# Chunk attention that takes 512 queries at once for each block of keys, with the score work moved to other steps

## The chip, the cores and the metric

The kernel runs on one core of one Trainium2 chip. The metric is the time of one execution on the device, in microseconds (us). Of three timed executions of the kernel before, the median is 1950.27 us (1949.37 to 1955.56); a fourth execution was taken with the hardware profiler and is the one whose trace is read below.

Engines are named as in the profile: PE is the matrix engine (PEld its loading of stationary operands), DVE, ACT and POOL are the vector, scalar and general engines, SP issues most of the transfers. Each works through its own queue in order, and waits there on semaphores.

## The reference, cut to what matters

One layer of a streaming encoder for 2048 positions of width 1024, all in float32: RMSNorm, one wide input projection, two gated branches (chunk-causal attention with 8 heads of 64; retention with 8 heads), a gated merge, an output projection and a final RMSNorm. The change is in the attention alone. Per head, a query in chunk n (chunks of 64) sees the keys of chunks n-8 to n:

```
dist = q_local[:, None] + N_LEFT_CHUNKS * CHUNK - p[None, :]
bias = rel_bias[:, clip(dist, -REL_CLIP, REL_CLIP) + REL_CLIP]
s = einsum('nqhd,nkhd->nhqk', qc, k_band) * scale + bias[None]
s = where(valid, s, NEG_INF)
w = softmax(s, axis=-1)
o = einsum('nhqk,nkhd->nqhd', w, v_band)
```

So a tile of 128 queries (two chunks) sees at most 640 keys, that is five blocks of 128; a block of 128 keys is seen by five such tiles in a row, at most four of which lie in one block of 512 queries.

## The kernel before, in words

**Precision.** Every float32 operand is split into a high and a low part of type fp32r ("h" and "l" in the names), and a product is two or three matmuls on the parts. In the attention a score tile is two matmuls per range of columns (`wide` from `qa` and `ka`, whose rows hold both parts), and the product of weights and values is two (`po` from `pth` and from `ptl`, both with the stationary operand `va`, in which the value's two parts stand side by side).

**Stages.** Projection of the first 1024 positions, attention and retention of the first half (`heads(0)`), projection of the second half, `heads(1)`, then merge and output. Between the attention's and the retention's own matmuls the program puts dense projection work: `fill(n)` takes n steps of a stream of dense work, and a step is three matmuls of 512 columns (`ps_g_...` in the trace of attention). `later(n, fn)` hands the rest of a task to the n-th step from now, where it is emitted ahead of that step's matmuls. So the order in every engine's queue is the order in which this program emits, and no scheduler changes it.

**Attention before.** `attention(s, ...)` runs once per half. Its unit is a head h, a block b of 512 positions and a half `un` of 256 queries: 32 units in each call. A unit does:

- `soft` twice (a = 0, 1), each for 128 queries: the scores go into one of two places in the PSUM tile `wide` (three banks of 512 columns; columns 128 to 767 and 768 to 1407, so the middle bank holds some of each). Then `least` one step later (DVE: bias added and the minimum taken, result in `pr`, row minimum in `mn`), `exps` two steps later (ACT: exponential and row sum), `normed` four steps later (DVE reciprocal, POOL scales `pr`). `pr` has four buffers (`PR_BUFS`).
- `weighted` for the unit before: three groups of two key blocks each. A group transposes the 128x128 pieces of `pr` on PE (`tp`, one of four PSUM banks that the dense work uses too), copies them to `pth` (ACT), writes the rest to `ptl` (DVE, a step later), and three steps later (`PV_LAG`) multiplies: per key block, values stationary, 256 columns of weights moving, for `pth` and `ptl`. Of the six key blocks the first and the last are seen by one of the two query tiles only, and there the other 128 columns of `pth` and `ptl` are set to zero on DVE.
- after a block's second half, `out_`: ACT copies the low half of `po` to `oa`, DVE adds the high half, POOL multiplies with the gate `ua`, and SP stores it. `po` is one bank.

The order of a unit is: scores a = 0, two steps, scores a = 1, one step, then group, step, group, step, group, step of the unit before. For block 0 there are no earlier keys: one group and two groups, and scores of 128 to 512 columns.

Loads are issued by SP (`load_q`, `load_k`, `load_vs`, `load_u`), one unit ahead for the queries. Tiles of the pool `e` (`E(...)`: `qa`, `va`, `ua`, `pth`, `ptl`, `oa`) share twelve buffers (`E_ATT`); a tile waits until the one that had its buffer is no longer used.

The functions that the change touches, with the line numbers of the profile (instructions recorded through a helper have its line, L143, in the trace):

## Time and profile before

| | us |
|---|---|
| timed executions, median (range) | 1950.27 (1949.37 to 1955.56) |
| the profiled execution, own time | 1955.26 |
| its span, first to last instruction | 1953.5 |
| PE busy in the span | 1889.6 (97%) |
| PEld / DVE / ACT / POOL busy | 1624.6 / 1358.5 / 931.6 / 971.0 |
| attention of the first half, first scores to last product | about 354 to 568 |
| attention of the second half | about 1102 to 1349 |

The columns of the views: a row of the timeline has the start and the busy time in us, the engine, the line, the operation, out<-in by the program's names, the shape of the output and how many instructions of one kind follow each other. Matmuls are pipelined: a matmul's shown time is longer than the distance to the next one, so what a matmul costs is read from the starts of neighbouring rows. A gap shorter than that overlap does not show up as idle time. In a row of a group, the count is followed by busy time and mean duration, and by the engine's idle time just before such instructions with what ended it.

### The profile page before, as it was taken

How to read it: one execution, taken by the hardware profiler on the slowest of the kernel's cores; microseconds unless marked ns; L12 is line 12 of the kernel's file. 1: busy time of each engine (PE TensorE's matmuls, PEld its weight loads, DVE VectorE, ACT ScalarE, POOL GpSimd, SP SyncE). 2: the span in 40 equal slices, each digit the busy share in tenths (PEclk: the TensorE clock that was granted, in tenths of full speed). 3: DMA queues.
4: the chain of work that ended last, by engine and by line, in shares of the span. 5: the costliest groups of instructions: out<-in, count | busy, mean ns of one | idle time of the engine just before them, and what ended most of it. 6: DMA issues, size and time to landing. Idle time of an engine off the chain costs nothing. (4 is left out here: it accounts for less than half of the span.)

```text
span 1953.5 us, 31945 instructions
## 1 busy us (share of the span) xinstructions
PE 1889.6 (97%) x10437; PEld 1624.6 (83%) x10437; DVE 1358.5 (70%) x2473; ACT 931.6 (48%) x1931; POOL 971.0 (50%) x790
## 2 busy tenths in 40 slices
PE   7999989999999999999989999999999999999998
PEld 6889879888888887799879888888888878887886
DVE  6878788677766558888788677765455655557655
ACT  7545554566655445343333566664455321223554
POOL 0425545555545565535455454554554114557775
PEclk9999999999999999999999999999999999999999
DMA  6585976656559978665765555654999899977673
GB/s 194 154 259 194 283 251 212 195 173 187 168 161 282 277 226 278 201 224 181 221 226 190 178 158 164 179 162 134 267 273 275 302 370 333 313 265 246 205 233 134
DMA packets 325557, 435.93 MB, mean 223 GB/s; under 512 B 29880, under 2 KB 191184, under 8 KB 325392
## 3 DMA queue, kind: packets, MB, share of 16 engines
q1 hardware_dynamic: 260096, 368.35, 58.9%
q10 hardware_dynamic: 65296, 65.55, 11.0%
q8 instruction: 83, 1.36, 0.3%
q14 instruction: 82, 0.67, 0.1%
HBM read 288.14 MB, written 145.64 MB: 222 GB/s over the span
## 5 line engine op out<-in xcount | busy, mean ns | idle before, releaser
L143 POOL TENSOR_SCALAR pr<-pr,rsum 128x640 f32<-128x640 f32 (+4 forms) x128 | 96.1, 751 | 212.5 <-DVE ptl L143 104.9
L143 PE MATMUL ps_g_z<-r,wh_g 128*128 128x512 f32 x448 | 145.3, 406 | 1.9 <-DVE c_g L143 1.9
L143 PE MATMUL ps_g_x<-r,wh_g 128*128 128x512 f32 x448 | 144.6, 404 | 1.0 <-ACT u_g L143 0.9
L143 DVE CUSTOM_DVE_ANT_0 pr<-wide,bt 128x640 f32<-128x640 f32 (+4 forms) x128 | 94.2, 736 | 61.8 <-PE wide L143 53.6
L143 ACT ACTIVATE pr<-pr,mn 128x640 f32<-128x640 f32 (+4 forms) x128 | 98.0, 766 | 80.9 <-DVE mn L143 80.9
L143 DVE TENSOR_TENSOR ptl<-tp,pth 128x384 fp32r<-128x384 f32 x168 | 96.0, 572 | 41.5 <-ACT pth L143 39.0
L143 ACT CAST pth<-tp 128x384 fp32r<-128x384 f32 x168 | 84.5, 515 | 68.2 <-PE tp L143 65.3
L143 POOL TENSOR_TENSOR sl<-sm,sh 128x384 fp32r<-128x384 f32 x64 | 68.2, 1065 | 62.9 <-ACT sh L143 44.8
L143 ACT CAST wh_p<-raw_p 128x512 fp32r<-128x512 f32 x111 | 68.3, 619 | 63.1 <-PE ps_p_v L143 16.6
L143 DVE TENSOR_TENSOR wl_p<-raw_p,wh_p 128x512 fp32r<-128x512 f32 x111 | 91.5, 835 | 8.7 <-ACT wh_p L143 8.7
L143 POOL TENSOR_TENSOR wl_g<-t_g,wh_g 128x512 fp32r<-128x512 f32 x56 | 75.1, 1341 | 39.5 <-ACT wh_g L143 39.2
L143 PEld LDWEIGHTS tp<-ident,pr 128*128 128x128 f32 x560 | 71.1, 140 | 27.6 <-POOL pr L143 3.1
L143 DVE TENSOR_TENSOR sm<-sr,dm 128x384 f32<-128x384 f32 x64 | 35.5, 555 | 82.8 <-PE sr L143 28.5
L143 PE MATMUL po<-pth,va 128*128 128x256 f32 x336 | 92.4, 295 | 0.0
L143 PE MATMUL tp<-ident,pr 128*128 128x128 f32 x560 | 89.3, 272 | 3.0 <-POOL pr L143 1.7
L143 PE MATMUL wide<-ka,qa 128*128 128x384 f32 (+1 forms) x448 | 88.2, 313 | 2.2 <-DVE mn L143 2.1
L143 PEld LDWEIGHTS wide<-ka,qa 128*128 128x128 f32 x448 | 74.6, 188 | 18.6 <-DVE mn L143 8.7
L143 PE MATMUL po<-ptl,va 128*128 128x256 f32 x336 | 88.3, 284 | 1.4 <-DVE ptl L143 0.2
L143 PE MATMUL ps_g_z<-r,wl_g 128*128 128x512 f32 x224 | 89.0, 397 | 0.0
L143 PE MATMUL ps_g_x<-r,wl_g 128*128 128x512 f32 x224 | 88.8, 397 | 0.0
L143 PEld LDWEIGHTS ps_g_x<-r,wh_g 128*128 128x128 f32 x448 | 76.8, 191 | 10.8 <-ACT u_g L143 2.3
L143 PEld LDWEIGHTS ps_g_z<-r,wh_g 128*128 128x128 f32 x448 | 76.6, 191 | 10.4 <-issue 2.3
(930 smaller groups left out, 6293.5 us busy)
## 6 DMA issues: line engine op xcount, KB each, us to landing
raw_g<-in_w_in_dram ACTq DMA_DIRECT2D x56, 512.0 KB, 4.6
raw_p<-in_w_in_dram ACTq DMA_DIRECT2D x50, 512.0 KB, 5.7
qa<-qas SPq DMA_DIRECT2D x128, 128.0 KB, 3.4
qr<-qrs SPq DMA_DIRECT2D x128, 128.0 KB, 4.9
vr<-vrs SPq DMA_DIRECT2D x64, 256.0 KB, 5.4
ka<-kas SPq DMA_DIRECT2D x56, 256.0 KB, 3.3
va<-vas SPq DMA_DIRECT2D x40, 256.0 KB, 3.5
kds<-kdt_k SPq DMA_DIRECT2D x32, 256.0 KB, 3.9
```

The lines of the kernel that those rows point to most:

```text
L143: return tc.keep_in_program_order(op(*a, **k))
```

## The change

The unit of attention becomes a head and a whole block of 512 queries, 16 units in each call. The product of weights and values is done per key block for all query tiles that see it: with t the query tile (0 to 3) and j the key block (0 to 7, block 4 being the first of the unit's own positions), block j is seen by the tiles from max(0, j-4) to min(3, j), so its moving operand is 1, 2, 3, 4, 4, 3, 2, 1 pieces of 128 columns wide, and nothing is set to zero. Six groups: j = (0, 1), 2, 3, 4, 5, (7, 6), of 3, 3, 4, 4, 3, 3 transposes. For block 0 only the last three groups exist.

A unit is written as twelve slots, each followed by one step. Even slots hold a group of the current unit; slots 2, 6, 8 and 10 (`SOFT_AT`) hold the scores of the next unit's four tiles. The queries' first half for the next unit is loaded in slot 0 and the second in slot 3, keys two units ahead in slot 6, values and gate in slot 9. For a unit of block 0, slots 0, 1 and 4 have no step, and the unit before the first has none in slots 0 and 1. The first group's product comes four steps after its transposes, the others' three. `pr` has five buffers and is allocated at `least`, the pool `e` has eleven. The number of steps is the same as before: 198 in the first call, 222 in the second.

```diff
-E_ATT = 12
+E_ATT = 11
-PR_BUFS = 4
+PR_BUFS = 5
+SOFT_AT = (2, 6, 8, 10)
...
-        units = [(h, b, un) for h in range(HEADS) for b in (2 * s, 2 * s + 1) for un in range(2)]
+        units = [(h, b) for h in range(HEADS) for b in (2 * s, 2 * s + 1)]
...
-        def soft(h, b, un, a):
+        def soft(h, b, t):
...
-            pr = sbp.tile([P, WIN], F32, tag="pr", bufs=PR_BUFS, name=f"pr_{nm}")
...
             def least():
+                prs[h, b, t] = sbp.tile([P, WIN], F32, tag="pr", bufs=PR_BUFS, name=f"pr_{nm}")
...
-        def weighted(h, b, un, pr2):
...
+        def weighted(h, b, gr):
+
+            k0 = 0 if b > 0 else 4
+            js = ((0, 1), (2,), (3,), (4,), (5,), (7, 6))[gr]
+            tp = ACC(f"tp_{h}_{b}_{gr}")
+            c, cut, parts = 0, [], []
+            for j in js:
+                ts = range(max(0, j - 4), min(4, j + 1))
+                cut.append((j, c, ts))
+                for t in ts:
+                    at = (j - max(t, k0)) * P
+                    pe.transpose(tp[:, c:c + P], prs[h, b, t][:, at:at + P], ident)
+                    c += P
...
+            def product():
+                for j, at, ts in cut:
+                    n = len(ts) * P
+                    v4 = vts[h, b - 1 + j // 4][:, j % 4, :]
+                    for i, p in enumerate(parts):
+                        pe.matmul(
+                            po[:, ts[0] * P:ts[0] * P + n], v4, p[:, at:at + n],
+                            start=j == (0 if b > 0 else 4) and i == 0, stop=gr == 5 and j == 6 and i == 1,
+                            skip_group_check=True,
+                        )
+                if gr == 5:
+                    later(1, out_)
...
+            part("h")
+            later(1, lambda: part("l"))
+            later(PV_LAG + (gr == 0), product)
+
+        def slot(m, n):
+
+            if n == 0 and m + 1 < len(units):
+                h, b = units[m + 1]
+                load_q(h, b, 0)
...
+            if n == 3 and m + 1 < len(units):
+                load_q(*units[m + 1], 1)
+            if n == 6 and m + 2 < len(units):
+                load_k(*units[m + 2])
+            if n == 9 and m + 1 < len(units):
+                load_vs(*units[m + 1])
+                load_u(*units[m + 1])
+            if m >= 0 and n % 2 == 0:
+                weighted(*units[m], n // 2) if units[m][1] or n > 4 else None
+            if m + 1 < len(units) and n in SOFT_AT:
+                soft(*units[m + 1], SOFT_AT.index(n))
...
+        fill(2)
+        for m in range(-1, len(units)):
+            for n in range(12):
+                slot(m, n)
+                bare = (0, 1) if m < 0 else () if units[m][1] else (0, 1, 4)
+                fill(0 if n in bare else ATT_FILL)
+        fill(PV_LAG + 3)
```

Counted over the whole program, PE's queue loses 224 of its matmuls (`po` from 336 + 336 to 224 + 224) and DVE's loses 224 settings to zero; the count of every other kind of instruction is unchanged. Two places show how the order moves.

On PE, the product of one group in the second half: in the kernel before, block 3, first half of the queries, third group's transposes and the first group's product behind them.

```order
L143 MATMUL tp_3_0_2_14597<-ident,pr_3_1_14455 128x128
L143 MATMUL tp_3_0_2_14597<-ident,pr_3_0_14418 128x128
L143 MATMUL tp_3_0_2_14597<-ident,pr_3_1_14455 128x128
L143 MATMUL po<-pth_3_0_0_14567,va_2_14330 128x256
L143 MATMUL po<-ptl_3_0_0_14575,va_2_14330 128x256
L143 MATMUL po<-pth_3_0_0_14567,va_2_14330 128x256
L143 MATMUL po<-ptl_3_0_0_14575,va_2_14330 128x256
```

In the changed kernel, from the transposes of block 2's fifth group (`tp_2_4`) on: the scores of the next unit's third tile, then the product of the fourth group.

```order
L144 MATMUL tp_2_4_13789<-ident,pr_2_2_13609 128x128
L144 MATMUL tp_2_4_13789<-ident,pr_2_3_13648 128x128
L144 MATMUL wide<-ka_3_13559,qa_3_1_13718 128x384
L144 MATMUL wide<-ka_3_13559,qa_3_1_13718 128x256
L144 MATMUL wide<-ka_3_13559,qa_3_1_13718 128x384
L144 MATMUL wide<-ka_3_13559,qa_3_1_13718 128x256
L144 MATMUL po<-pth_2_3_13765,va_2_13622 128x512
L144 MATMUL po<-ptl_2_3_13775,va_2_13622 128x512
L144 MATMUL ps_g_3_z<-r_86,wh_g_3_4_13611 128x512
```

Two matmuls of 512 columns stand where four of 256 stood, and between a group's transposes and its product there is now the next pair of slots, scores included.

On DVE, the two minima (`ISA pr...<-wide,bt`) whose scores follow each other most closely: before, with what stands between them,

```order
L143 ISA pr_2_0_14629,mn_2_0_14630<-wide,bt_14200 128x640
L143 ISA mn_2_0_14630 128x1
L143 TENSOR_TENSOR c_g_4_14641<-ps_g_4_z,u_g_4_14561 128x512
L143 TENSOR_TENSOR wl_g_5_0_14579<-raw_g_5_0_14150,wh_g_5_0_14578 128x512
L143 SCALAR_TENSOR_TENSOR g_3_2_1_14643<-g_3_2_1_14643,c_g_4_14641 128x512
L143 ISA pr_2_1_14666,mn_2_1_14667<-wide,bt_14200 128x640
```

and in the changed kernel, tiles 1, 2 and 3 of block 3 (slots 6, 8 and 10 of the unit before it):

```order
L144 ISA pr_3_1_13777,mn_3_1_13771<-wide,bt_13071 128x640
L144 ISA mn_3_1_13771 128x1
L144 TENSOR_TENSOR u_g_3_13787<-ps_g_3_v,u_g_3_13590 128x512
L144 TENSOR_TENSOR wl_g_3_6_13746<-raw_g_3_1_13019,wh_g_3_6_13745 128x512
L144 TENSOR_TENSOR ptl_2_4_13804<-tp_2_4_13789,pth_2_4_13793 128x384
L144 ISA pr_3_2_13806,mn_3_2_13799<-wide,bt_13071 128x640
L144 ISA mn_3_2_13799 128x1
L144 RECIPROCAL rsum_3_1_13772<-rsum_3_1_13772 128x1
L144 TENSOR_TENSOR ptl_2_5_13839<-tp_2_5_13825,pth_2_5_13829 128x384
L144 ISA pr_3_3_13841,mn_3_3_13835<-wide,bt_13071 128x640
```

A `ptl` now stands directly ahead of each of these minima, since a group and a score tile share the slot; before, the same step held no group. On ACT the exponentials and the `pth` copies alternate in the same way: exponential of tile 1, `pth` of group 4, exponential of tile 2, `pth` of group 5, exponential of tile 3.

More of the change, by code (lines that the diff above doesn't have):

```diff
@@ L1470, in turn_bias @@
             later(0, far)
-        def soft(h, b, un, a):
-            t = 2 * un + a
+        def soft(h, b, t):
+            un, a = divmod(t, 2)
             nm = f"{h}_{b}_{t}"
@@ new lines, in weighted, with part @@
+        def weighted(h, b, gr):
[10 more added lines that the diff above has]
+                    c += P
+            def part(which):
+                p = E(f"pt{which}_{h}_{b}_{gr}", F32R)
+                parts.append(p)
+                if which == "h":
+                    act.copy(p[:, 0:c], tp[:, 0:c])
+                else:
+                    dve.tensor_tensor(p[:, 0:c], tp[:, 0:c], r32(parts[0][:, 0:c]), ALU.subtract)
+            def product():
[10 more added lines that the diff above has]
+                    later(1, out_)
@@ L1575, in attention @@
         load_bias(0)
-        load_k(0, 2 * s)
-        load_q(0, 2 * s, 0)
+        load_k(*units[0])
         fill(12)
         turn_bias(0)
-        fill(6)
-        for m in range(len(units) + 1):
-            if m < len(units):
-                h, b, un = units[m]
-                if m + 1 < len(units):
-                    h2, b2, un2 = units[m + 1]
-                    load_q(h2, b2, un2)
-                if un == 0 and m + 2 < len(units):
-                    load_k(*units[m + 2][0:2])
-                if un:
-                    load_u(h, b)
-                if (b, un) == (2 * s, 0) and h + 1 < HEADS:
-                    load_bias(h + 1)
-                if (b, un) == (2 * s + 1, 0) and h + 1 < HEADS:
-                    turn_bias(h + 1)
-                prs[m] = [soft(h, b, un, 0)]
-                fill(2 * ATT_FILL)
-                prs[m].append(soft(h, b, un, 1))
-                fill(ATT_FILL)
-            if m:
-                for _ in weighted(*units[m - 1], prs.pop(m - 1)):
-                    fill(ATT_FILL)
-            if m < len(units) and un == 0:
-                later(PV_LAG - 1, lambda h=h, b=b: load_vs(h, b))
```

57 lines of the change are left out of this document (7 added, 50 removed).

## The prediction

> **What bounds the kernel now.** I read the page first, for how full PE is, then each attention call by itself, then what PE waited for.
>
> ```profile
> span 1953.5 us, 31945 instructions
> PE 1889.6 (97%) x10437; PEld 1624.6 (83%) x10437; DVE 1358.5 (70%) x2473; ACT 931.6 (48%) x1931; POOL 971.0 (50%) x790
> ```
> ```profile
> 354.00:568.00 214.00, 211.80 (x1232) 179.88 (x1231) 157.11 (x457) 135.27 (x316) 117.53 (x132) 1.00 0.58 173
> 1102.00:1349.00 247.00, 243.83 (x1467) 210.99 (x1467) 179.69 (x494) 149.42 (x325) 119.26 (x120) 1.00 0.53 159
> ```
> ```profile
> PE wide L143 <- DVE mn L143: 2.1, 2, 1.3
> PE tp L143 <- POOL pr L143: 1.7, 2, 1.0
> ```
>
> The two window rows are the attention calls, their columns the length, then busy time of PE, PEld, DVE, ACT and POOL, the granted clock (full) and DMA. PE is busy for 211.8 of 214 and 243.8 of 247 us, while DVE is at 73% in both. The visible waits that belong to the attention are a few us in all. So in both calls the matmuls set the time, and a matmul less is time less; other engines count only where PE comes to wait for them. Waits below a matmul's pipelined length hide in the busy time, so the timeline has to be read by starts:
>
> ```profile
> 1143.38 0.49 PE L143 MATMUL tp<-ident,pr 128*128 128x128 f32 x3
> ...
> 1144.40 0.60 PE L143 MATMUL tp<-ident,pr 128*128 128x128 f32 x4
> 1144.75 0.71 PE L143 MATMUL ps_g_z<-r,wh_g 128*128 128x512 f32 x2
> 1145.30 0.39 PE L143 MATMUL ps_g_z<-r,wl_g 128*128 128x512 f32 x1
> 1145.53 0.49 PE L143 MATMUL tp<-ident,pr 128*128 128x128 f32 x3
> 1145.79 0.36 PE L143 MATMUL po<-pth,va 128*128 128x256 f32 x1
> 1146.25 0.39 PE L143 MATMUL po<-ptl,va 128*128 128x256 f32 x1
> 1146.47 0.28 PE L143 MATMUL po<-pth,va 128*128 128x256 f32 x1
> ...
> 1146.71 0.62 PE L143 MATMUL ps_g_z<-r,wh_g 128*128 128x512 f32 x2
> 1147.17 0.40 PE L143 MATMUL ps_g_z<-r,wl_g 128*128 128x512 f32 x1
> 1147.40 0.75 PE L143 MATMUL wide<-ka,qa 128*128 128x384 f32 x4
> 1147.99 0.28 PE L143 MATMUL po<-pth,va 128*128 128x256 f32 x1
> ```
>
> Prices from the starts. A step, three matmuls of 512, is 1147.40 - 1146.71 = 0.69, so 512 columns cost 0.23. 256 columns cost 0.12 (two in 1146.71 - 1146.47). A score tile (two of 384, two of 256) is 0.59, so 384 cost about 0.175. Four transposes are 0.35, and the pair of 512 behind takes 0.55 where 0.46 is usual, so 0.44 with the switch back; three are 0.25 + 0.09 = 0.34.
>
> A lost place: the first `po` at 1145.79 is followed only after 0.46, where 0.12 and the 0.09 of the switch would do. So 0.25 is lost, waiting for DVE's `ptl`, with no idle time shown.
>
> **The change, part by part.** The sum is made against the profiled execution's own 1955.3 us; the median of the timed runs is 1950.3, 5 lower, and the same difference is taken off that.
>
> *1. Fewer and wider products.*
>
> ```profile
> L143 PE MATMUL po<-pth,va 128*128 128x256 f32 x336 | 92.4, 295 | 0.0
> ```
> ```profile
> 1939.29 2.72 PE ps_out_z L143 x12
> 1942.01 1.43 PE ps_out_x L143 x12
> ```
> ```profile
> 481.90 0.33 PE L143 MATMUL wide<-ka,qa 128*128 128x128 f32 x2
> 482.07 0.33 PE L143 MATMUL po<-pth,va 128*128 128x256 f32 x1
> 482.25 0.28 PE L143 MATMUL po<-ptl,va 128*128 128x256 f32 x1
> ```
>
> The last chain gives sharper prices: twelve of 512 in 2.72 us (0.227 each), twelve of 256 in 1.43 (0.119). Before there are 336 products with `pth` and as many with `ptl`, all 256 wide: 672 x 0.119 = 80.0 us. After, a unit with b > 0 has two matmuls for each of eight key blocks, 16 where 24 stood, and one of block 0 has 8 for 12: over 24 and 8 units 448 matmuls, 112 each of 128, 256, 384 and 512 columns. The price of 128 is the open one. The rows show two of 128 and one of 256 in 482.25 - 481.90 = 0.35, which leaves 0.115 each if the third costs its usual 0.119. But the two alone move the start by 0.17 only, and 0.06 is what a quarter of a 512 takes; these are the bounds. I take 0.115, because the late start of the next matmul belongs to them. After: 112 x (0.115 + 0.119 + 0.175 + 0.227) = 71.2 us. **Term: -8.8 us**; with 0.06 it would be -15.
>
> *2. Transposes and scores* keep number and grouping (groups of 3 and 4, four switches of 3 and two of 4 per block): nothing.
>
> *3. The hidden waits for `ptl`.* Twelve places like 1145.79 lie between these two:
>
> ```profile
> 374.72 0.36 PE L143 MATMUL po<-pth,va 128*128 128x256 f32 x1
> 375.23 0.39 PE L143 MATMUL po<-ptl,va 128*128 128x256 f32 x1
> ...
> 1339.36 0.35 PE L143 MATMUL po<-pth,va 128*128 128x256 f32 x1
> 1339.82 0.39 PE L143 MATMUL po<-ptl,va 128*128 128x256 f32 x1
> ```
>
> They come where three groups follow each other step by step: the group transposed at 1143.38 has its product at 1145.79, 2.4 us on. In the new order the shortest such distance is 3.0 us (slot 10: transposes 0.34, scores 0.59, a product of two 384s 0.35, two steps 1.38, the next transposes 0.34), the others 3.2 to 3.8. The groups of the second call give what the work takes (mean ns after the busy time):
>
> ```profile
> L143 DVE CUSTOM_DVE_ANT_0 pr<-wide,bt 128x640 f32<-128x640 f32 x59 | 48.4, 821 | 38.3 <-PE wide L143 34.9 <-issue 1.3 <-POOL pr L143 1.2
> L143 ACT ACTIVATE pr<-pr,mn 128x640 f32<-128x640 f32 x59 | 49.1, 833 | 45.0 <-DVE mn L143 45.0
> L143 ACT CAST pth<-tp 128x384 fp32r<-128x384 f32 x62 | 29.9, 482 | 34.3 <-PE tp L143 31.5 <-issue 2.7
> L143 ACT CAST pth<-tp 128x512 fp32r<-128x512 f32 x31 | 18.0, 580 | 0.0
> L143 DVE TENSOR_TENSOR ptl<-tp,pth 128x384 fp32r<-128x384 f32 x62 | 31.9, 514 | 5.0 <-ACT pth L143 4.6
> L143 DVE TENSOR_TENSOR ptl<-tp,pth 128x512 fp32r<-128x512 f32 x31 | 21.4, 691 | 18.4 <-ACT pth L143 16.5 <-POOL pr L143 1.6
> L143 ACT ACTIVATION_READ_ACCUMULATOR pr<-pr,mn 128x1 f32 x59 | 11.2, 189 | 0.0
> L143 DVE RECIPROCAL rsum<-rsum 128x1 f32<-128x1 f32 x60 | 7.3, 121 | 0.0
> L143 POOL TENSOR_SCALAR pr<-pr,rsum 128x640 f32<-128x640 f32 x60 | 48.1, 801 | 124.6 <-DVE ptl L143 73.7 <-DVE rsum L143 50.7
> L143 ACT CAST wh_g<-t_g 128x512 fp32r<-128x512 f32 x27 | 16.5, 611 | 0.0
> L143 DVE MEMSET pth<- 128x128 f32 x62 | 10.2, 165 | 0.0
> ```
>
> `pth` and `ptl` are 1.0 to 1.3 us plus queueing, and the 224 zero settings of 0.165 leave the queue that was late. **Term: -3.0 us** (12 x 0.25); if none goes, 0. They were off PE's path elsewhere, so the 37 us of DVE time count no further.
>
> *4. The ends of the two calls.* The two waits of `tp` for POOL, 1.7 us together, are the last unit's, which has no scores beside it to wait behind. In the new order the last tile's reciprocal and scaling are emitted with slot 1's step and its first transpose stands in slot 4, three steps and a group later (2.4 us, against 0.12 for the reciprocal and 0.80 on POOL). **Term: -1.7 us.**
>
> *5. A new tight place: scores behind scores.* Both places of `wide` use the middle PSUM bank, so tile 2's scores (slot 8) wait until DVE has taken tile 1's minimum (slot 6), and tile 3's (slot 10) for tile 2's. Behind a waiting score stand all of PE's matmuls. Before, two steps and two products, 2.3 us, lay between such neighbours, and in DVE's queue no `ptl` of the same step. Now one group stands ahead of each minimum. From slot 6's transposes on: `pth` from 0.6 to 1.2 us, `ptl` to 1.9, minimum to 2.75; the exponential (0.83, and about half of the 0.19 that reading its sum shows) to 3.75, and only then, in ACT's order, `pth` of slot 8 to 4.25, `ptl` to 4.75, minimum to 5.6. PE reaches slot 8's scores at 0.44 + 0.59 + 0.45 + 1.38 + 0.34 = 3.2 and slot 10's at 3.2 + 0.59 + 0.45 + 1.38 + 0.34 = 5.95. So 0.35 us is to spare at the second place when nothing else is in the chain, and in a unit of block 0, where no product lies in slots 6 and 7, PE is 0.45 earlier and loses about 0.15. Of the 23 units with full-wide scores whose orders I went through, four have one ACT instruction of about 0.6 between exponential and `pth` (0.35 lost each), two have two, which wait for DVE besides (1.3 each). DVE's own two dense instructions fit into its wait for ACT. That gives 4 x 0.35 + 2 x 1.3 + 8 x 0.15 = 5.2. Lower bound 0 (semaphores as quick as assumed, queues ahead), upper 23 (24 units, each with one ACT instruction of 0.6 and one DVE instruction of 0.7 in the chain, less the 0.35 to spare). **Term: +5.2 us.** The Trainium skill says that software has to guard PSUM by bank and quadrant and not by address (PSUM — Partial Sum Buffer, PSUM bank collisions raise a hardware error). By that rule the wait is needed though the two score places share no column; the two waits of `wide` in the rows above, 2.1 us, agree.
>
> *6. Query loads.*
>
> ```profile
> DMA to landing us min/median/max: 2.4/3.4/6.8
> ```
>
> The first half of the queries is now issued in slot 0 for slot 2, where six steps lay between. But SP does not wait for PE's place: its buffer comes free with the product of group 3, in slot 8 of the unit before, four slots and 6 us of PE ahead of the use. Two pieces of 3.4 us, 0.6 us apart, land in that. Only at the start of each call, where the load follows fourteen steps that it used to precede, may up to 1 us be lost. **Term: +0.5 us** (0 to 2; a late 6.8 us landing is in it).
>
> Sum: -8.8 - 3.0 - 1.7 + 5.2 + 0.5 = **-7.8 us**: the profiled execution would take 1947.5 and the median of runs about **1942.5 us** (-0.40%).
>
> **The rivals.**
>
> *A narrow product costs its columns.* Two of 128 moved the start by only 0.17 us. If the rest was the switch of operands and 128 costs 0.06, term 1 is -15, the sum -14: 1936. Against it speaks that PEld is busy for 83% and that the next start is late. The Trainium skill's gap of N/2.4 + 2.5 ns for matmuls in a row (TensorE: Matmul & The Clock Gate, Back-to-back issue gap) says 56 ns for 128 columns, which would go with this rival; its 109 and 216 ns for 256 and 512 are near the rows' 119 and 227.
>
> *The chain of term 5 takes the gain.* If each of 24 units loses 0.4 us there, +9.6 stands for +5.2, and with terms 3 and 4 half as large (-2.4 for -4.7) the sum is -1.2: 1949, no measurable difference. For it: ACT already waits 45.0 us for `mn`, and now `pth` stands in the same series. Against: DVE idles 34.9 us waiting for scores, so it is ahead as a rule.
>
> *The same chain, past its point: slower.* With 0.9 us per unit (an ACT and a DVE instruction in the chain each time, 0.6 + 0.7 less what is to spare) it costs 21.6 us against 8.8 + 3.0 + 1.7 = 13.5, and term 6 adds 0.5: 1959. It decides from 0.55 us per unit on, and is measurable from 0.8. That needs dense instructions in the chain in nearly all units, where the order shows six.
>
> *The products do not get fewer.* The order has 448 of them in the widths above, so this has no chance of its own.
>
> **How the numbers follow.** Forecast case, 1938 to 1946: 0.52. Narrow products cheap or the chain without loss, 1931 to 1938: 0.14. Gain taken, 1946 to 1955: 0.22. Slower, above 1956: 0.12. A measurement of this kernel can tell about 0.3% (5.9 us) from no change. Below 1944.4 lie the second case and some nine tenths of the first (0.60); above 1956.1 lies 0.12; 0.28 between. For 8 in 10 the range goes from 1933 to 1955.
>
> **What would show each step.** Four groups of `po`, 112 each; a row of two of 128 followed by one of 256 in 0.35 (0.115) or in 0.24 (0.06). No gaps of 0.46 between `po` rows. At the calls' ends no `tp` idle for POOL. Tight place: PE idle before `wide` with a DVE minimum as releaser, above all the second of two score tiles 2.8 us apart; under 6 us in all is the forecast, 10 to 20 the rivals. `wide` idle for DMA at the start of the calls would be term 6. The forecast is wrong if the attention calls (214 and 247 us) do not shorten by about 3 and 5.

## The result

The changed kernel takes 1971.63 us, the median of 5 runs (1966.99 to 1974.83), against 1955.26 us of the kernel before in the same session (5 runs, 1949.37 to 1960.72). The ratio is 1.0092, with a 95% interval from 1.0073 to 1.0111: slower by about 0.9%, where 0.4% faster was forecast; 1971.6 lies outside the range of 1933 to 1955.

### The profile after

First the page of the changed kernel, its span and the busy times of the engines.

```profile
span 1969.2 us, 31239 instructions
PE 1887.2 (96%) x10213; PEld 1610.0 (82%) x10213; DVE 1339.6 (68%) x2249; ACT 934.4 (47%) x1931; POOL 974.5 (49%) x790
```

There are 224 matmuls less, as the change says, and PE is busy for 2.4 us less (1889.6 before), but the span is 15.7 us longer. So PE stands idle where it did not. Where it does is read from the windows of the two attention calls, from the first score to the last product. The columns are those of the prediction. The prediction's second window was wrong: it began at 1102, while the second call of the kernel before begins at 1087.2, so it lacked 15 us. Both calls again, of the kernel before:

```profile
354.50:567.72 213.22, 211.02 (x1229) 179.26 (x1228) 156.61 (x456) 134.77 (x316) 117.03 (x132) 1.00 0.59 174
1087.20:1348.42 261.22, 256.78 (x1540) 222.09 (x1539) 189.56 (x520) 157.39 (x343) 126.45 (x128) 1.00 0.53 159
```

and of the changed kernel:

```profile
349.50:588.82 239.32, 220.02 (x1159) 181.78 (x1160) 150.83 (x362) 139.51 (x320) 118.55 (x135) 0.99 0.53 157
1104.40:1365.02 260.62, 257.76 (x1439) 219.32 (x1440) 179.37 (x395) 159.26 (x347) 134.39 (x132) 1.00 0.53 162
```

The change also draws nine dense steps more into each call: 27 matmuls, 6.1 us at 0.227. Without them the second call is 260.6 - 6.1 - 261.2 = **6.7 us shorter**, more than was forecast for it, and the first is 239.3 - 6.1 - 213.2 = **20.0 us longer**. All else together is 2.4 longer (15.7 = 20.0 - 6.7 + 2.4). Nearly the whole loss lies in the first call, the only one with units of block 0. PE idles there for 239.3 - 220.0 = 19.3 us, against 2.2 before. The waits of PE in that window, in us together, number, longest:

```profile
PE wide L144 <- DMA qa<-qas: 7.5, 4, 2.5
PE tp L144 <- POOL pr L144: 5.9, 7, 1.5
PE po L144 <- DVE oa L144: 2.7, 5, 0.9
PE wide L144 <- DVE mn L144: 2.2, 3, 1.1
```

**Scores wait for queries.** All four load waits are those of the first score tile of a block-1 unit, in slot 2 of a block-0 unit, whose slots 0 and 1 have no step. What SP issued ahead of one of them, in the timeline, and what it stood at between 397 and 411:

```profile
397.38 0.43 SPq L144 DMA_DIRECT2D urs<-g  x1
405.40 1.09 SPq L144 DMA_DIRECT2D qa<-qas  x2
406.54 1.06 SPq L144 DMA_DIRECT2D ka<-kas  x2
407.64 0.47 SPq L144 DMA_DIRECT2D oas<-oa  x1
408.21 0.53 SPq L144 DMA_DIRECT2D va<-vas  x1
408.78 0.49 SPq L144 DMA_DIRECT2D ua<-uas  x1
409.31 0.60 SPq L144 DMA_DIRECT2D urs<-g  x1
410.32 3.28 SPq L144 DMA_DIRECT2D qa<-qas  x4
```
```profile
SPq L144 <- POOL oa L144: 7.5, 1, 7.5
SPq L144 <- PE po L144: 0.3, 1, 0.3
```
```profile
415.89 0.82 PE L144 MATMUL wide<-ka,qa 128*128 128x384 f32 x4 [1.70 <-DMA qa<-qas]
```

The load of 405.40, a second query half, had got the buffer of gate factors that POOL was still to multiply with. SP stood there for 7.5 us; then eight transfers left in 5 us. Behind them SP waited another 0.3 us for a product of PE, and at 410.32 the query half left that PE needed next; its score began 5.6 us later. So what set the moment of 410.32 was this last wait and not the long one; the long one made the transfers leave in a bunch.

**Transposes wait for POOL.** The first group of a block-0 unit reads all four score tiles; its fourth transpose is the late one:

```profile
388.87 0.49 PE L144 MATMUL tp<-ident,pr 128*128 128x128 f32 x3
390.88 0.33 PE L144 MATMUL tp<-ident,pr 128*128 128x128 f32 x1 [1.52 <-POOL pr L144]
```

**Products wait for the product bank.** The bank holds a block's whole product, as before, but the next unit's first product now comes three steps behind the last one, where it came four behind, and it waits until DVE has added the bank's halves, in both calls:

```profile
1212.73 0.33 PE L144 MATMUL po<-pth,va 128*128 128x128 f32 x1 [0.26 <-DVE oa L144]
```

### The profile page after: what moved, and what is told of

Its sections match the earlier page's. It is cut to its first block, busy times and chain, and to the rows that moved or that the text cites. A ratio compares the mean times of both kernels' runs of the same rounds, so it can differ in the third digit from the quotient of the medians.

```text
span 1969.2 us, 31239 instructions
## 1 busy us (share of the span) xinstructions
PE 1887.2 (96%) x10213; PEld 1610.0 (82%) x10213; DVE 1339.6 (68%) x2249; ACT 934.4 (47%) x1931; POOL 974.5 (49%) x790
## 5 line engine op out<-in xcount | busy, mean ns | idle before, releaser
L144 DVE TENSOR_TENSOR ptl<-tp,pth 128x512 fp32r<-128x512 f32 (+1 forms) x168 | 100.4, 598 | 109.0 <-ACT pth L144 98.9
L144 PE MATMUL wide<-ka,qa 128*128 128x384 f32 (+1 forms) x448 | 98.1, 335 | 11.4 <-DMA qa<-qas 7.5
L144 ACT CAST pth<-tp 128x512 fp32r<-128x512 f32 (+1 forms) x168 | 85.2, 507 | 42.4 <-PE tp L144 31.5
L144 PEld LDWEIGHTS ps_g_x<-r,wh_g 128*128 128x128 f32 x448 | 81.3, 191 | 15.6 <-ACT u_g L144 2.3
L144 PEld LDWEIGHTS ps_g_z<-r,wh_g 128*128 128x128 f32 x448 | 80.9, 190 | 15.9 <-issue 2.3
L144 POOL TENSOR_TENSOR t_g<-raw_g,t_g 128x512 f32<-128x512 f32 x56 | 73.0, 1303 | 27.8 <-issue 12.1
L144 PEld LDWEIGHTS wide<-ka,qa 128*128 128x128 f32 x448 | 67.6, 191 | 18.1 <-DVE mn L144 5.4
L144 PE MATMUL po<-pth,va 128*128 128x512 f32 (+1 forms) x224 | 75.5, 350 | 4.6 <-DVE oa L144 4.6
## 6 DMA issues: line engine op xcount, KB each, us to landing
vr<-vrs SPq DMA_DIRECT2D x64, 256.0 KB, 5.3
ka<-kas SPq DMA_DIRECT2D x56, 256.0 KB, 3.5
va<-vas SPq DMA_DIRECT2D x40, 256.0 KB, 2.9
kds<-kdt_k SPq DMA_DIRECT2D x32, 256.0 KB, 3.9
```

Of the source, the lines that this page charges most:

```text
L144: return tc.keep_in_program_order(op(*a, **k))
```

## The experiments

Every kernel was timed beside the kernel before, whose median was 1950.8 to 1955.3 us in the five sessions; the ratio is to that, so compare ratios, not medians. "First" and "second" are the lengths of the two calls in the profiled execution, "rest" what its span leaves. The rest is of one execution: the changed kernel, e2, e4 and e9 do the same work there and show 1464.5 to 1471.4.

| kernel | median us | ratio, 95% | first | second | rest |
|---|---|---|---|---|---|
| before | 1955.3 | 1 | 213.2 | 261.2 | 1479.1 |
| changed | 1971.6 | 1.0092 [1.0073, 1.0111] | 239.3 | 260.6 | 1469.3 |
| e1 | 1981.4 | 1.0144 [1.0117, 1.0170] | 250.4 | 260.5 | 1466.8 |
| e2 | 1973.0 | 1.0109 [1.0088, 1.0129] | 243.4 | 260.2 | 1470.5 |
| e3 | 1968.7 | 1.0087 [1.0067, 1.0106] | 238.3 | 260.2 | 1468.1 |
| e4 | 1974.0 | 1.0115 [1.0094, 1.0135] | 241.3 | 262.7 | 1464.5 |
| e5 | 1963.2 | 1.0056 [1.0038, 1.0073] | 233.7 | 259.8 | 1469.3 |
| e6 | 1958.6 | 1.0035 [1.0020, 1.0051] | 231.0 | 259.7 | 1463.4 |
| e7 | 1962.4 | 1.0049 [1.0035, 1.0064] | 230.5 | 259.7 | 1470.4 |
| e8 | 1953.0 | 1.0006 [0.9993, 1.0018] | 227.9 | 255.8 | 1471.4 |
| e9 | 1962.7 | 1.0029 [1.0013, 1.0044] | 240.1 | 255.4 | 1471.4 |
| e10 | 1958.0 | 1.0021 [1.0009, 1.0033] | 217.1 | 262.0 | 1481.0 |
| e11 | 1950.4 | 0.9986 [0.9969, 1.0002] | 229.2 | 256.0 | 1460.4 |
| e12 | 1946.5 | 0.9952 [0.9937, 0.9967] | 228.5 | 255.0 | 1463.3 |
| e13 | 1955.1 | 1.0013 [0.9998, 1.0027] | 229.7 | 258.8 | 1468.7 |
| e14 | 1962.0 | 1.0046 [1.0030, 1.0062] | 238.3 | 255.0 | 1462.4 |
| e15 | 1942.2 | 0.9941 [0.9918, 0.9964] | 219.9 | 257.1 | 1459.9 |
| e16 | 1939.8 | 0.9937 [0.9915, 0.9958] | 221.0 | 255.3 | 1462.3 |

The first call holds 534 dense matmuls in the changed kernel, 558 (5.4 us more) where a block-0 unit has one more step (e1, e3, e7, e8, e12 to e16).

### Single causes: a step more, an earlier load, narrower products

Run e1 gives slot 4 of a block-0 unit a dense step:

```diff
-                bare = (0, 1) if m < 0 else () if units[m][1] else (0, 1, 4)
+                bare = (0, 1) if m < 0 else () if units[m][1] else (0, 1)
```

> The changed kernel, but slot 4 of a block-0 unit also gets a dense step (eight steps more in the first attention call, taken from the work that follows it). Theory A, crowded block-0 units: with slots 0, 1 and 4 without a step, PE reaches the first transposes of a block-0 unit (which read all four score tiles) before POOL has scaled the fourth tile; one more step (0.69 us) ahead of them takes about that much from each of the seven waits of transposes for POOL (5.9 us in all, the longest 1.5), so about 1.5 us of them is left, the four waits of scores for query loads (7.5 us) stay as they are, and the time falls by 4 to 5 us. Theory B, late query loads set the pace of these units: the time that PE saves at slot 4 comes back as longer waits for the loads, and the time stays within 2 us. Theory C, the tight chain of scores (term 5): the waits of scores for DVE minima (2.6 us) do not move, the time stays.

Run e2 loads the first query half two slots sooner:

```diff
             if n == 0 and m + 1 < len(units):
                 h, b = units[m + 1]
-                load_q(h, b, 0)
...
+            if n == 10 and m + 2 < len(units):
+                load_q(*units[m + 2], 0)
...
         load_k(*units[0])
+        load_q(*units[0], 0)
         fill(12)
```

> The changed kernel, but the first half of a unit's queries is loaded two slots earlier (in slot 10 of the unit two before, ahead of two steps instead of none, and for the very first unit ahead of the fourteen steps). Theory B, the load is issued too late: the four waits of scores for query loads (7.5 us) fall below 1.5 us, the stretch at half clock behind the longest of them goes too (about 3 us in all), and 7 to 10 us go. Theory A: PE then comes earlier to the transposes of the same units, whose waits for POOL grow from 5.9 towards 11 us (1.4 each, as in the units that had no load wait), so only 3 to 5 us go. If the load is held by its buffer or by what stands ahead of it in SP's queue, and not by its place, the waits for loads stay near 7 us and the time stays within 2 us.

Run e3 makes both edits:

> Both edits together: a step in slot 4 of the block-0 units and the earlier load of the first half of the queries. If A and B are two causes side by side, the first call's idle time (19.5 us) falls to 7 or less (5.0 of it the waits for the minimum and for the evacuation of the product bank) and the time falls by 11 to 15 us, to about 1957 to 1961, level with the kernel before. If only B counts, it is as fast as the early load alone; if only A, as the step alone.

PE's waits for queries in e1, e2 and e3, in this order:

```profile
PE wide L144 <- DMA qa<-qas: 15.9, 10, 3.2
```
```profile
PE wide L144 <- DMA qa<-qas: 9.7, 4, 2.8
```
```profile
PE wide L144 <- DMA qa<-qas: 6.0, 5, 1.9
```

In e1 the waits for POOL are gone from the page, but those for queries have doubled, and it is slower than the changed kernel (the intervals do not touch). So a step more is no mending: what PE saves ahead of the transposes it pays at the loads, as theory B said, and more (4.2 us of it between the calls, in a wait that e7 shows). But B fails in e2: the earlier place brought nothing (9.7 for 7.5). The load got another buffer that was also held: at the place shown above it left 2.2 us ahead of PE's being ready for the score (413.98 for 416.2), where in the changed kernel it left 3.9 ahead (410.32 for 414.2). What stands in a load's way is its buffer and SP's order. Neither edit alone helps, and e3 gains a little at best (its interval overlaps that of the changed kernel).

Run e4 cuts the products to 256 columns:

```diff
-                        pe.matmul(
-                            po[:, ts[0] * P:ts[0] * P + n], v4, p[:, at:at + n],
...
+                        for x in range(0, n, 256):
+                            y = min(n, x + 256)
+                            pe.matmul(
+                                po[:, ts[0] * P + x:ts[0] * P + y], v4, p[:, at + x:at + y],
...
```

In the block-0 units both pieces of the first product carry the start flag, so part of their output differs; the work is the same.

> The changed kernel with its products cut again into pieces of at most 256 columns (512 as two of 256, 384 as 256 and 128): 672 matmuls instead of 448, nothing else changed. Term 1 as predicted: 112 x (0.115 + 0.119 + 0.234 + 0.238) = 79.1 us against 71.2, so 7.9 us slower than the changed kernel where products lie on the path throughout, and some 1 to 2 us less than that if the longer products fill waits in the block-0 units. Rival, the width does not matter, or the narrow product costs its columns (0.06): 5 us slower or less.

The second call grows by 2.1 us for the 4.5 of its share. Its waits for the product bank fell from 1.9 to 0.9 meanwhile, so a part of the longer products ran where PE had waited anyway. This left term 1 open until e13.

### Who holds the buffers

Run e5 loads values and gate factors later:

```diff
-            if n == 9 and m + 1 < len(units):
-                load_vs(*units[m + 1])
-                load_u(*units[m + 1])
+            if n == 9 and m + 1 < len(units) and s and units[m + 1][1] == 2:
+                load_v(units[m + 1][0], 1)
+            if n == 3 and m >= 0:
+                load_v(*units[m])
+            if n == 9 and m >= 0:
+                load_u(*units[m])
```

> The changed kernel, but a unit's values are loaded in its own slot 3 and its gate factors in its own slot 9, six and twelve slots later than in the change (both still six steps or more ahead of their use); the queries stay where they are. Theory D, buffers and SP's order: a query half got the buffer that gate factors still held for POOL's last multiplication, SP stood there 7.5 us, and the loads behind it left in a bunch, the next unit's first query half last. With the two loads later, fewer of the eleven buffers are held, SP's waits for POOL's multiplication (65 us in the first call) fall below 35, the scores' waits for query loads from 7.5 to 3 us or less, and the time by 4 to 6 us. Theory B, place of the load alone: nothing changes, since the query loads stand where they stood. Theory A: at most 2 us, the rest comes back as waits of the transposes for POOL.

Run e6 adds the early first query half of e2, one slot sooner still (slot 9):

> As the run before it, and the first query half loaded three slots sooner (slot 9 of the unit two before). Theory D: the earlier place counts now that a free buffer is there for it, where the early load alone had made things worse: waits for query loads 1 us or less, 7 to 9 us faster than the changed kernel if little comes back as waits of transposes for POOL (5.9 us in the changed kernel). Theory A: these grow to 8 to 11 us, and the gain stays at 3 to 4 us.

PE's waits for POOL and for queries in the first call, for e5 and then e6 (no row for queries is left in e6):

```profile
PE tp L144 <- POOL pr L144: 5.9, 5, 2.0
PE tp L144 <- DMA qa<-qas: 0.6, 1, 0.6
```
```profile
PE tp L144 <- POOL pr L144: 6.5, 6, 2.0
```

The first call is 5.6 and 8.3 us shorter than in the changed kernel, the kernel about 0.36 and 0.57% faster than the changed one. The late values and gate factors alone take the waits for queries from 7.5 to 0.6 us. What the early load adds in e6 is not clear of noise in time (the intervals of e5 and e6 overlap); it does no harm any more. SP still stood for POOL's multiplication for 49.9 us in e5, where below 35 had been expected. But in e5 all 15 of these waits stand ahead of stores, which need the multiplied output; in the changed kernel six, with 43.3 of 65.2 us, stood ahead of query loads.

Run e10 puts the taken buffer alone into the kernel before:

```diff
-E_ATT = 12
+E_ATT = 11
-PR_BUFS = 4
+PR_BUFS = 5
```

> The kernel before with one part of the change alone: eleven buffers for loads and weights and five for the scores, where there were twelve and four. Theory D1, the buffer that was taken away is what makes the loads late: scores of the kernel before then wait for query loads too, 3 to 8 us in the first call, and it is 0.2 to 0.5% slower than the kernel before. Theory D2, the number is not it, the change holds the buffers longer (gate factors loaded twelve slots sooner, values six): no load waits, the same time within 0.15%.

It is 0.21% slower, so D2 as written fell; but no score waits for queries there. The 4 us more of its first call are other waits, of products for the lower weights above all:

```profile
PE po L143 <- DVE ptl L143: 2.0, 4, 0.8
```

So the number of buffers has a price of its own, and the late queries of the changed kernel go with how long they are held.

### Cover, and where it is taken from

Run e7 adds to e6 a step in slot 1 of the block-0 units:

```diff
-                bare = (0, 1) if m < 0 else () if units[m][1] else (0, 1, 4)
+                bare = (0, 1) if m < 0 else () if units[m][1] else (0, 4)
```

> As the run before it, and a dense step in slot 1 of the block-0 units (eight steps more in the first call). If D and A are two causes that must both go, the waits of transposes for POOL fall to 3 us or less and no load wait takes their place, unlike in the run with a step in slot 4, which got slower: 10 to 14 us faster than the changed kernel, 1958 to 1962. If D alone counts, as the run before it.

The waits for POOL fell to 1.5 us and no load wait came; without its 5.4 us of dense work the first call is 5.9 us shorter than in e6. But the time did not fall: the rest grew by 7 us, though it has 5.4 us less to do. Between the calls, at the step from retention to the next projections, PE now waits for ACT, in e7 (first row) as in e8, where e6 and the changed kernel have 1.5 and 1.4. Around and behind this wait, which ended at 779.70, the granted clock of e7 was 0.52 from 777.0 to 784.1 us. What else grew there is not explained.

```profile
PE ps_p_x L144 <- ACT u_p L144: 6.9, 2, 6.3
```
```profile
PE ps_p_x L144 <- ACT u_p L144: 7.4, 2, 6.7
```

Run e8 takes ACT's part of the evacuation a step sooner:

```diff
                 if gr == 5:
-                    later(1, out_)
+                    out_()
```

> As the run before it, and ACT takes the upper half of a finished product bank in the step of the last product, one step sooner. The waits of the next unit's first product for DVE's addition (4.6 us seen, and 0.15 us unseen at each of the other places) should fall to 1 us or less, 4 to 6 us faster than the run before it, 1953 to 1957, level with the kernel before. If ACT, which now stands behind the last product, comes late to the next group's weights, the gain is half of that or less.

In e8 no product waits for the bank any more, in either call, and its ratio is 0.43% below that of e7, more than the 4 to 6 us expected. Run e9 does this edit alone in the changed kernel:

> The changed kernel with one edit alone: ACT takes the upper half of a finished product bank in the step of the last product, one step sooner. Theory E, the product bank: one bank holds a unit's whole product now, and PE waits for its evacuation at nearly every unit, seen (4.6 us) or inside a matmul's pipelined length. Then the second call, which has no load waits, gets shorter by 3 to 5 us (260.6 in the changed kernel); in the first call most of the gain goes into the waits for late loads, so 3 to 6 us in all. If only the seen waits count, the second call gains 2 us, and all of it 2 to 4.

The second call of e9:

```profile
1107.40:1362.82 255.42, 254.89 (x1438) 220.06 (x1439) 177.71 (x395) 159.22 (x347) 135.38 (x132) 1.00 0.54 165
```

5.2 us less (3.9 in e8, against e7), where 1.9 us had been seen as waits: two thirds of this price were hidden inside the matmuls' pipelined length. In the first call of e9 all of it went into the late loads (12.1 us of waits for queries, from 7.5), as theory E said. The timed gain, 0.6%, is more than the 3 to 6 us expected and more than the 2.3 us by which its profiled span is shorter; that execution was the slowest of its five.

Run e11 is e8 without the step in slot 1; run e12 is e8 with eight steps less ahead of the call:

```diff
         load_k(*units[0])
         load_q(*units[0], 0)
-        fill(12)
+        fill(4)
         turn_bias(0)
```

> Late values and gate factors, early first query half, early evacuation of the product bank; slots 0, 1 and 4 of the block-0 units without a step, as in the changed kernel. Theory F, dense work that is pulled into the attention is missing later: the wait of 6.7 us of the dense products for ACT's gate factors between the two calls, which the runs with a step more had (and the others not), is gone again, and the time is 1950 to 1954, 2 us or more faster than the same kernel with the step in slot 1, though 3 to 5 us of waits for POOL's scaled weights come back in the first call. If the step in slot 1 is worth its work, 1955 to 1958.

> As the run with the step in slot 1 and the early evacuation, but with eight dense steps less ahead of the first scores (4 for 12), so that as much dense work is left behind the first call as in the changed kernel. Theory F: the waits of the block-0 units for POOL stay at 3 us, the wait of 6.7 us between the calls goes, and the time is 1946 to 1951, 2 to 7 us faster than that run and level with or up to 0.2% faster than the kernel before. If the dense work ahead of the call is as useful where it was (loads and bias of the first head come too late with 6 steps of lead), the first unit waits 2 to 5 us, and the time is that of the run with the step.

In both the wait of 6.7 us between the calls is gone (1.5 and 1.6 us for `u_p`). Without the step, e11 has 6.5 us of waits for POOL, where 3 to 5 had been expected, and in time it cannot be told from e8. With the lead moved, the block-0 units keep their cover (1.3 us of waits for POOL), and e12 beats the kernel before by 0.48%. Theory F holds in every run as far as the wait goes: it is 5.5 to 7.4 us in the four kernels with a step more and the full lead (e1, e3, e7, e8), and 1.4 to 1.6 in all others. What makes ACT late there was not followed further.

### The mended kernel: terms 1 and 5 by themselves

Run e13 cuts the products of e12 as e4 did (with one start flag only). Run e14 puts the change's loads back into e12. Runs e15 and e16 place its scores in other slots:

```diff
-SOFT_AT = (2, 6, 8, 10)
+SOFT_AT = (1, 4, 7, 10)     e15
+SOFT_AT = (2, 5, 8, 11)     e16
```

> The mended kernel (late values and gate factors, early first query half, early evacuation, step in slot 1, less lead) with its products cut into pieces of at most 256 columns: 672 matmuls for 448. Term 1 as predicted: where products lie on the path, 7.9 us slower than the mended kernel (1954), 4.5 of them in the second call, whose length goes from 255.0 to 259.5. Rival: the cut products fill waits here too, 2 to 4 us slower in all and 2 in the second call, as in the changed kernel.

> The mended kernel with the loads of the change: values and gate factors in slot 9 of the unit before, the first query half in slot 0. Theory D: scores wait for query loads again, 6 to 15 us in the first call, and it is 8 to 14 us slower than the mended kernel; the second call stays at 255. Rival: with a step in slot 1 ahead of the scores and less lead the old loads come in time, at most 3 us slower.

> The mended kernel with the four score tiles in slots 1, 4, 7 and 10, three slots apart, for 2, 6, 8 and 10. Term 5: the waits of scores for the minimum (7.2 us in the first call, all but one in slot 8 of a block-0 unit, two slots behind the tile before) fall below 2 us, and it is 4 to 6 us faster than the mended kernel, unless the transposes of the first key blocks then catch on the scaled weights. Rival: DVE as a whole is late in the block-0 units, the wait goes to another score tile or to the products, and the time stays within 2 us.

> The mended kernel with the score tiles in slots 2, 5, 8 and 11: the same distances, but the fourth tile one slot later than now. Term 5: the waits for the minimum fall below 2 us as in the run before; the fourth tile's scaled weights come a slot later, so that in the block-0 units the transposes wait 0.5 to 1 us each for POOL (4 to 8 us in all), and the time is that of the mended kernel within 3 us. If the distance of the scores alone decides, as fast as the run before.

The second call in e12 and in e13:

```profile
1080.50:1335.52 255.02, 254.94 (x1439) 219.96 (x1438) 179.19 (x398) 159.71 (x349) 134.24 (x130) 1.00 0.54 169
```
```profile
1081.10:1339.92 258.82, 258.73 (x1568) 226.83 (x1567) 179.40 (x398) 160.32 (x349) 134.25 (x130) 1.00 0.54 167
```

3.8 us for the 4.5 of term 1, in a call where nothing else changed; 1.2 in the first, where waits for the minimum shrank by 2.7. In time e13 is 0.61% slower than e12, some 12 us, of which the calls show 5; the rest lies where the two kernels do the same, and is not explained.

The old loads (e14) cost 9.8 us in the first call of the mended kernel, and 0.94% in time:

```profile
PE wide L144 <- DMA qa<-qas: 8.8, 5, 2.9
```

The waits for the minimum in the first call of e12, then e15, then e16:

```profile
PE wide L144 <- DVE mn L144: 7.2, 10, 2.3
```
```profile
PE wide L144 <- DVE mn L144: 0.7, 1, 0.7
```
```profile
PE wide L144 <- DVE mn L144: 1.8, 3, 0.8
```

With scores three slots apart the first call is 8.6 and 7.5 us shorter. In e15 the second call gives back 2.1 us; in e16 the transposes wait 0.5 us for POOL where 4 to 8 had been expected. In time neither can be told from e12 (0.9941 and 0.9937 against 0.9952, with intervals that overlap); both are 0.6% faster than the kernel before.

## Why the prediction was wrong

**Term 6 failed first.** It put the query loads at +0.5 us, because the buffer "comes free with the product of group 3, in slot 8 of the unit before, four slots and 6 us of PE ahead of the use". That the buffer frees with a product was right, but the 6 us are those of an ordinary unit. In a block-0 unit slots 0 and 1 hold neither a step nor a group, which leaves four steps (2.8 us), transposes (0.34), scores (0.59) and one group's products (0.35): some 4 us at the prediction's own prices, with nothing to spare for its two pieces of 3.4 us, 0.6 apart. The traces say the same: at each of the four waits the load left 3.9 us before PE was ready for the score (410.32 for 414.2). How long PE then waited followed from the landing, here of the load of 381.49, which another block-0 unit needed, and of that of 410.32:

```profile
DMA to landing us min/median/max: 3.6/3.7/3.7
```
```profile
DMA to landing us min/median/max: 4.9/5.0/5.0
```

Behind the first the score waited 0.3 us (put down to `u_g` by the profile); at the four waits, of 1.1 to 2.5 us, the loads took 4.3 to 5.8 us. They left in the bunch behind the buffer of gate factors, which the change loads twelve slots sooner and which the prediction did not mention. That it is the bunch that makes them land late is likely and was not tested by itself. Measured: 7.5 us of waits seen in the changed kernel, 0.6 with values and gate factors loaded late (e5), and 9.8 us of call length where the old loads alone are put back into a mended one (e14 against e12).

**Term 4** was right for the place that it named: the waits of `tp` at the end of the calls are gone. But it took the last unit as the only one that has too little beside it. Each block-0 unit, with its three empty slots, is another; the mechanism of this term then costs 5.9 us, seven times, against a gain of 1.7.

**A term was missing: the product bank.** That the bank has to be evacuated between two units, now within three steps for four, is in the diff, and was costed nowhere. e9 puts it at 5.2 us in the second call. The Trainium skill says that independent groups of matmuls should rotate through different PSUM banks, so that the evacuation of one overlaps the matmuls of the next (Perfetto Trace Analysis, Matmuls). The rows of `po` waiting for `oa` agree; with one bank for it, an earlier evacuation did as well.

**Terms 1 and 3 held.** In the second call, with the late work taken out (e12), the call is 255.0 - 6.1 - 261.2 = 12.3 us shorter than before. Of this, 256.8 + 6.1 - 254.9 = 8.0 are PE's busy time, where 5.0 were forecast for the products (384 x 0.119 - 64 x 0.636) and 2.3 for the nine of term 3's twelve places that lie in this call. The other 4.3 are idle time of the kernel before; term 4 had named 1.0 of it, and the rest (1.3 for a minimum, 1.1 for `ptl` ahead of transposes) stood in no term: part of it lay in the 15 us that the prediction's window left out. e13, with 3.8 for 4.5, shows term 1 by itself. The price of a product of 128 columns, the open one, can be read in the changed kernel, at two places:

```profile
386.34 0.22 PE L144 MATMUL po<-pth,va 128*128 128x128 f32 x1
386.40 0.27 PE L144 MATMUL po<-ptl,va 128*128 128x128 f32 x1
386.51 0.34 PE L144 MATMUL po<-pth,va 128*128 128x256 f32 x1
386.68 0.28 PE L144 MATMUL po<-ptl,va 128*128 128x256 f32 x1
...
1208.76 0.31 PE L144 MATMUL po<-pth,va 128*128 128x128 f32 x1
1208.90 0.28 PE L144 MATMUL po<-ptl,va 128*128 128x128 f32 x1
1209.01 0.33 PE L144 MATMUL po<-pth,va 128*128 128x256 f32 x1
1209.19 0.28 PE L144 MATMUL po<-ptl,va 128*128 128x256 f32 x1
```

The first of 128 takes 0.06 at one place and 0.14 at the other, the second 0.11, the 256 behind them 0.17 and 0.18. With 0.12 for the last, the four take 0.46 and 0.55, where 0.47 was forecast and 0.36 would be the rival's, a narrow product that costs its columns. So the rival is out, and the price of 0.115 was right or a little low. The gap of 56 ns that the Trainium skill gives for 128 columns (TensorE: Matmul & The Clock Gate, Back-to-back issue gap) is near the 0.06 of the first place, and the other three distances are twice that or more.

**Term 5** had the mechanism, and as long as other waits came first, its size (2.2 us in the first call, 0.5 in the second, 5.2 forecast). It named block-0 units too, but at 0.15 us each; in e12, with the other waits mended, this chain cost 7.2. The rivals with the same chain in every unit did not come: the second call shows it once. One reading was too quick: of the two waits of `wide` that were to agree with the rule of banks, the one that ended at 1091.89 lies between neighbours in the middle bank, but at 358.02 a score for columns 0 to 383 waited for a minimum over columns 1024 to 1279, which share no bank. So these rows do not show that it is the bank that counts. **Term 2** stands: scores and transposes kept their number.

**Outside the calls** the prediction assumed nothing. Drawing 54 dense matmuls into the calls should have left 12.2 us less to do there; the rest fell by 9.8. With 24 more drawn in it fell no further (e7). Both differences from the work drawn in, 2.4 and 6.5 us, lie within the 7 us by which executions with the same work there differ.

In sum, a gain of the size of -8.8 - 3.0 - 1.7 was there to be had: e16 is 0.63% faster than the kernel before, some 12 us. That the two are so near is in part luck, since the second call alone gives 255.3 - 6.1 - 261.2 = -12.0 and waits went that stood in no term. In the changed kernel the units of block 0 took the gain back. The prediction read them as ordinary units with fewer products, and asked what is missing in their slots in one term out of six.

## What to carry to other kernels

When a schedule is rewritten, go through its shortest unit, not the ordinary one: follow every buffer, score and bank through the slots that hold no cover, and in the issuing queue also what stands ahead of a load. A load issued sooner helps only if its buffer is free by then, so look at who holds buffers longer than before. Dense work that covers one place is missing at another: e7 mended most waits of its target, and lost the gain behind the call.

## What the runs showed of the hardware

Waits of PE can cost more than their length. Behind the wait of 1.70 us that ended at 415.89 the granted clock (the third column from the right) fell to half for 3.4 us:

```profile
413.87:417.28 3.41, 1.71 (x12) 1.38 (x11) 1.82 (x6) 2.28 (x8) 1.15 (x3) 1.00 0.83 276
417.28:420.69 3.41, 3.41 (x10) 2.53 (x9) 1.24 (x5) 2.61 (x5) 2.65 (x3) 0.50 0.57 195
```
```profile
418.04 1.05 PE L144 MATMUL ps_g_x<-r,wh_g 128*128 128x512 f32 x2
418.90 0.63 PE L144 MATMUL ps_g_x<-r,wl_g 128*128 128x512 f32 x1
```

Two matmuls of 512 took 418.90 - 418.04 = 0.86 us there, 0.43 each for 0.23, so 3.4 us at half clock cost 1.7 us. The same came with the wait of 2.54 us that ended at 533.62, but not with the one of 2.13 us that ended at 446.20:

```profile
441.17:444.59 3.42, 2.90 (x15) 2.14 (x13) 3.03 (x8) 2.19 (x6) 2.12 (x2) 1.00 0.87 236
444.59:448.00 3.41, 1.80 (x11) 1.72 (x12) 0.83 (x2) 1.49 (x6) 0.88 (x3) 1.00 1.00 260
```
```profile
529.92:533.34 3.42, 1.16 (x6) 0.62 (x4) 1.81 (x5) 2.12 (x4) 0.38 (x1) 1.00 0.95 308
533.34:536.75 3.41, 3.13 (x11) 2.97 (x12) 0.93 (x4) 1.75 (x7) 1.24 (x4) 0.50 0.45 143
```

The two falls begin 533.34 - 417.28 = 116.06 us apart, which is 34 times 3.413, and all eight falls before the end of the work begin on one such grid; the rows above are windows of that grid. Ahead of each of the eight PE was idle for 1.7 to 2.6 us of the window. The wait that ended at 446.20 was cut by an edge of the grid at 444.59, which left 0.5 us of idle time in one window and 1.6 in the next. So what fits these rows is how much of a wait falls into one window, and not its length alone. How much it takes is not settled: one window of this trace (from 1806.51) passed with 1.8 us idle and no fall.

The Trainium skill lets the clock fall after an idle window of about 3.4 us, and says that this window runs freely (TensorE: Matmul & The Clock Gate, What's actually happening). The trace agrees with a freely running window of that length. It differs in how much of it has to be idle: 1.7 us, half of it, were enough at 417.28.
